# Raising the scheduling priority of the RWKV recurrence steps in a hybrid decoder layer

## Chip, cores and metric

The kernel runs on one core of a Trainium2 chip. The metric is the device time of one execution in microseconds (us); the median of three runs of the kernel before is 1586.47 us (1586.15 to 1588.06).

## What is computed

One decoder layer over 1024 tokens of width 1024, in float32. An RMS norm and one input projection feed two branches: RWKV-7 time mixing (16 heads of 64) and dilated windowed attention (16 heads of 64). Both are gated, concatenated, projected out and added to the input; a last RMS norm follows. Cut to what matters:

```python
xn = rms_norm(h, norm_w)
p = einsum('bsd,dn->bsn', xn, w_in)              # 1024 x 8320
def step(state, inp):                            # the RWKV recurrence, per head, state 64 x 64
    r_t, w_t, k_t, v_t, av_t, bv_t = inp
    sa = einsum('bhvk,bhk->bhv', state, av_t)
    state = state * w_t + sa[..., None] * bv_t + v_t[..., None] * k_t
    return state, einsum('bhvk,bhk->bhv', state, r_t)
y_rwkv = gated(group_norm(lax.scan(step, s0, xs)))
y_att = mixed_dilated_attention(p[..., ATT0:ATT_GATE0], p[..., ATT_GATE0:])
h = h + einsum('bsm,md->bsd', concat([y_rwkv, y_att]), w_out)
return rms_norm(h, final_norm_w)
```

## The kernel before

The program has three stages. In the first (to about 880 us) the RWKV branch is computed, and the projections run beside it; then comes attention, with the remaining projections beside it; last comes the output projection.

**Units and chunks.** The RWKV stage works on 16 units: 8 pairs of heads, each in two halves of 512 tokens. A unit has 8 chunks of 64 tokens. The recurrence inside a chunk is turned into matrix products, for which a triangular matrix per chunk is inverted (`invert`); what is left of the recurrence is a serial chain over the chunks (`chain`), with three steps a chunk.

- `first`: a product of the state `Sd` closes the PSUM tile `z` (I write z<-Sd), DVE copies one half of it into the tile `zd` and then ACT the other (`spread`, L654 and L655). Two more products (T<-Vd, T<-Sd) open the chunk's result tile `T`.
- `second`: the product with the inverse `U` (z<-zd); DVE and then ACT write `ud` (L657, L658).
- `third`: T<-ud closes `T`; DVE and then ACT write the next state `Sd` (L657, L658), and z<-Vd opens the next chunk's `z`.

So one chunk is the loop z<-Sd, zd, z<-zd, ud, T<-ud, Sd, in which each link waits for the one before: three products on PE (in float32, 128 columns or fewer, two passes each) and three pairs of small operations on DVE and ACT, the one on ACT after the one on DVE.

**What lies beside the chain.** While unit p goes through its chain, unit p+1 is inverted (the columns on DVE at L568 and L570, a round trip through DRAM, then the small products m1 to m4 at L596, L606, L619 and L628) and unit p+2 is prepared (decay, norms, products `pa`). Unit p-1 is finished (group norm, gate). And PE has a stream of projection products, `pq` (L187), 128x512 in float32r, 3,120 of them in all, which wait for nothing in this stage: `advance(4)` takes four of them after every slot. A unit has 24 slots, one chain step in each; other steps are assigned to slots by the tables PREP, FIN, LATE, MS.

**What sets the order.** The loop below writes out the work slot by slot. A scheduler then fixes, when the program is built, one order for each engine's queue: it takes instructions that it holds to be ready, and among these the one with the highest priority, which without further word is the place in the written order. On the chip each engine works through its queue in that order and waits by semaphores. In a slot the chain step is written first, then `finish`, `late`, `invert`, `prepare`, `products`, then four `pq`.

Of the kernel before, what the change touches and what calls it, by code (L numbers as in the profile page):

```python
# [29 lines left out]
ATTG0 = 7296  # L30
NSLOT = 3 * NC_
AHEAD = 120
OFILL = 8
WARM = (4, 0)
V_AT = (-2, 3, -1)
# [18 lines left out]
class Kern:  # L54
# [135 lines left out]
    def stream(self, jobs):  # L190
# [3 lines left out]
        for i, (_, halves, take) in enumerate(jobs):  # L194
# [9 lines left out]
                yield  # L204
            w = wn

    def advance(self, n):
        for _ in range(n):
            next(self.flow, None)
        self.taken += n  # L210
# [80 lines left out]
    def rwkv(self, pairs=range(NPAIR), apairs=range(NPAIR)):  # L291
        nc = self.nc
        with ExitStack() as ctx:
# [45 lines left out]
            get = lambda n: units[n] if 0 <= n < N else None  # L339
            self.lora_w(units[0])  # L340
            for p in range(-2, N):
                dA, dI, dC, dF = get(p + 2), get(p + 1), get(p), get(p - 1)
                ev = [[] for _ in range(NSLOT)]
                put = lambda steps: [ev[s].append(f) for s, f in steps]
                if dC:
                    put(enumerate(self.chain(dC, get(p + 1) if dC["h"] == 0 else None)))
                if dF:
                    put(self.finish(dF))
                if dI:
                    put(self.late(dI))  # L350
                    put(self.invert(dI, self.Us[(p + 1) % 2]))
                if dA:
                    lag = WARM[p + 2] if p < 0 else 0
                    put([(n + lag, f) for n, f in self.prepare(dA) + self.products(dA)])
                if get(p + 3) and get(p + 3)["h"] == 0:
                    ev[12].append(lambda d=get(p + 3): self.lora_w(d))
                elif get(p + 3):
                    get(p + 3)["lw"] = get(p + 2)["lw"]
                if p == -2:
                    px = self.prep_x(1, self.lng, tags, ba)  # L360
                    for s in range(4):
                        ev[s].append(lambda: [next(px, None) for _ in range(2)])
                    ev[4].append(lambda: [None for _ in px])
                n = 5 if p < 0 else 2 if dA is not None and get(p + 3) is None else 4
                for s in range(NSLOT):
                    for f in ev[s]:
                        f()
                    self.advance(n)
# [367 lines left out]
    def attention(self, ctx, pairs=range(NPAIR), filler=None):  # L736
# [15 lines left out]
        per = 8 * 3 * KT  # L752
        done, ahead = max(0, self.taken - self.nrwkv), min(AHEAD, per * (len(prs) - 1))

# [26 lines left out]
        for j, (pr, e) in enumerate(heads):  # L781
            nxt = heads[j + 1] if j + 1 < len(heads) else None
            todo = self.scores(nxt[1], data[nxt[0]]) if nxt else []
            if j == len(heads) - 2:
                done, rate, per, ahead = 0, OFILL, 0, -20 * OFILL * (len(prs) - 1)
                self.flow = filler if filler is not None else iter(())
# [313 lines left out]
```

## Time and profile before

| | us |
|---|---|
| median of 3 runs | 1586.47 |
| the profiled execution, its own time | 1586.58 |
| its span, first to last instruction | 1584.9 |
| PE busy in the span | 1492.5 |
| PE busy from 140 to 840 us (chain of 15 of the 16 units) | 658.29 of 700 |
| DVE, ACT busy in that stretch | 474.32, 433.42 |

How to read it: PE is the matrix engine; its products are pipelined and their ends are modelled, so a product's row is longer than the time until the next may start. DVE and ACT are the vector and the scalar engine. "Idle before" and the views of waits name what ended an engine's idle time. An engine that is not the bottleneck may be idle at no cost.

### The profile page before, as it was taken

Reading aid. Unit: us, or ns where it says so; the run is one execution under the profiler, and the core shown is the slowest. Engines: PE = TensorE matmul, PEld = TensorE weight load, DVE = VectorE, ACT = ScalarE, POOL = GpSimd, SP = SyncE. Lnnn points to the kernel's source line nnn. Section 1 sums busy time; section 2 is a strip of 40 time slices with the busy share of each in tenths; the row PEclk is TensorE's granted clock in tenths of the full one; section 3 lists DMA queues with packets and bytes.
Section 4 is the critical chain, followed back from the end, with each engine's and each line's share of the span. In section 5 each row is a group of like instructions: output and inputs, shape, how many; then the busy total and the mean of one; then the engine's idle time right before and its main releaser. Section 6 shows DMA issues by size and latency. Waiting matters only on the chain.

```text
span 1584.9 us, 29112 instructions
## 1 busy us (share of the span) xinstructions
PE 1492.5 (94%) x10721; PEld 1211.0 (76%) x10721; DVE 1014.7 (64%) x2686; ACT 892.7 (56%) x2080; POOL 532.9 (34%) x668
## 2 busy tenths in 40 slices
PE   5889999999999999999999999999999999999997
PEld 4677777777777777777677788888888888787886
DVE  5866767677666676666743557676675766856234
ACT  5546666666656666566654456556565555645231
POOL 5443132222222221232211433443333334355542
PEclk9999999999999999999999999999999999999999
DMA  6121111111111111111111201111111111436452
GB/s 195 56 67 38 34 40 42 35 45 28 39 45 33 46 39 26 47 31 45 31 40 35 68 28 34 39 50 34 34 34 41 47 48 47 157 103 193 134 166 99
DMA packets 178829, 94.87 MB, mean 60 GB/s; under 512 B 58413, under 2 KB 164606, under 8 KB 178686
## 3 DMA queue, kind: packets, MB, share of 16 engines
q1 hardware_dynamic: 174942, 86.19, 19.6%
q10 hardware_dynamic: 3744, 6.82, 1.3%
q8 instruction: 84, 1.38, 0.4%
q14 instruction: 59, 0.48, 0.1%
HBM read 75.01 MB, written 17.83 MB: 59 GB/s over the span
## 4 chain that ended last, share of the span: by engine, by line
PE 66%; DVE 18%; ACT 9%; issue 4%; POOL 1%; DMA 1%; DVEq 0%; SPq 0%; ACTq 0%; POOLq 0%
PE pq L187 31%; PE oq L984 10%; PE T L643 4%; PE z L643 3%; PE o L930 3%; PE pa L527 2%; PE mp L857 2%; PE sp L890 2%; DVE I L422 1%; PE sp L910 1%; PE sp L909 1%; ACT zt L724 1%; DVE TB L568 1%; ACT ud L658 1%; DVE UB L570 1%
## 5 line engine op out<-in xcount | busy, mean ns | idle before, releaser
L187 PE MATMUL pq<-xh,wh 128*128 128x512 f32 x1040 | 430.6, 414 | 0.0
L187 PE MATMUL pq<-xl,wh 128*128 128x512 f32 x1040 | 414.7, 399 | 0.0
L187 PE MATMUL pq<-xh,wl 128*128 128x512 f32 x1040 | 291.8, 404 | 0.0
L179 POOL TENSOR_TENSOR wl<-wraw,wh 128x512 fp32r<-128x512 f32 x138 | 181.1, 1328 | 173.9 <-issue 46.3
L187 PEld LDWEIGHTS pq<-xh,wh 128*128 128x128 f32 x1040 | 197.0, 190 | 32.6 <-issue 0.2
L187 PEld LDWEIGHTS pq<-xl,wh 128*128 128x128 f32 x1040 | 197.4, 190 | 31.2 <-DVE xl L166 0.2
L187 PEld LDWEIGHTS pq<-xh,wl 128*128 128x128 f32 x1040 | 187.8, 190 | 33.0
L918 POOL TENSOR_TENSOR pl<-p,ph 128x512 fp32r<-128x512 f32 (+2 forms) x96 | 102.0, 1068 | 202.7 <-ACT ph L917 182.4
L984 PE MATMUL oq<-ow,qr 128*128 128x512 f32 x512 | 162.2, 395 | 1.2 <-ACT ow L965 0.6
L859 DVE CUSTOM_DVE_ANT_0 mp<-mp,maskq 128x512 f32<-128x512 f32 (+1 forms) x192 | 105.5, 570 | 68.0 <-PE mp L857 59.5
L913 ACT ACTIVATE p<-p 128x512 f32<-128x512 f32 (+2 forms) x144 | 64.6, 452 | 103.8 <-DVE p L912 103.0
L979 POOL TENSOR_TENSOR vr<-kr,qr 128x512 fp32r<-128x512 f32 (+2 forms) x68 | 90.4, 1335 | 80.9 <-ACT qr L978 74.0
L984 PEld LDWEIGHTS oq<-ow,qr 128*128 128x128 f32 x512 | 95.9, 188 | 23.0 <-ACT ow L965 1.0
L984 PE MATMUL oq<-ow,vr 128*128 128x512 f32 x256 | 101.2, 395 | 1.9 <-POOL vr L979 1.9
L178 ACT CAST wh<-wraw 128x512 fp32r<-128x512 f32 x138 | 79.7, 618 | 40.6 <-PE pq L187 30.9
L978 ACT CAST qr<-kr 128x512 fp32r<-128x512 f32 (+2 forms) x68 | 40.2, 594 | 94.3 <-PE oq L984 53.1
L912 DVE TENSOR_TENSOR p<-sp,maskt 128x512 f32<-128x512 f32 (+2 forms) x144 | 65.3, 457 | 42.9 <-PE sp L910 41.4
L643 PEld LDWEIGHTS T<-ud,TU 128*128 128x128 f32 x256 | 39.6, 188 | 56.2 <-ACT ud L658 51.8
L643 PE MATMUL T<-ud,TU 128*128 128x128 f32 x256 | 59.4, 314 | 22.7 <-ACT ud L658 22.1
L657 DVE TENSOR_SCALAR Sd<-T,dec 64x64 f32<-64x64 f32 x120 | 33.0, 275 | 66.8 <-PE T L643 65.0
L658 ACT ACTIVATE ud<-z,rn 64x64 f32<-64x64 f32 x128 | 39.4, 308 | 56.5 <-DVE ud L657 54.9
L658 ACT ACTIVATE Sd<-T,dec 64x64 f32<-64x64 f32 x120 | 36.9, 308 | 57.0 <-DVE Sd L657 55.6
(235 smaller groups left out, 3126.6 us busy)
## 6 DMA issues: line engine op xcount, KB each, us to landing
wraw<-in_w_in_dram SPq DMA_DIRECT2D x138, 256.0 KB, 3.0
kr<-mixd SPq DMA_DIRECT2D x60, 256.0 KB, 3.0
oraw<-in_w_out_dram SPq DMA_DIRECT2D x16, 512.0 KB, 5.2
xt<-in_x_dram SPq DMA_DIRECT2D x8, 512.0 KB, 3.8
ld<-TU SPq DMA_DIRECT2D x32, 128.0 KB, 2.7
mixd<-zt SPq DMA_DIRECT2D x16, 256.0 KB
mixd<-gt SPq DMA_DIRECT2D x16, 256.0 KB, 2.2
xr<-in_x_dram ACTq DMA_DIRECT2D x16, 256.0 KB, 2.8
```

The costliest lines, as they stand in the source:

```text
L178: nc.scalar.copy(out=wh[:, ks], in_=raw)
L179: nc.gpsimd.tensor_tensor(out=wl[:, ks], in0=raw, in1=wh[:, ks].bitcast(F32), op=ALU.subtract)
L187: return [lambda i=i, a=a, b=b: self.nc.tensor.matmul(q, lhsT=a, rhs=b, start=(i == 0), stop=(i == len(ops) - 1)) for i, (a, b) in enumera ...
L643: mm = lambda out, w, x, start, stop: nc.tensor.matmul(out, lhsT=w, rhs=f2(x), start=start, stop=stop, skip_group_check=True)
L658: S.activation(out=out[er[1], 1], in_=q[0:64, 64:128], func=AF.Copy, scale=scale[1])
L859: V.tensor_tensor_reduce(out=mp[:, :kn], in0=mp[:, :kn], in1=self.maskq[:, v0:v0 + kn], op0=ALU.add, op1=ALU.max, scale=1.0, scalar=-3e38, ...
L912: V.tensor_tensor(out=p[:, :qn], in0=sp[:, :qn], in1=self.maskt[:, u0:u0 + qn], op=ALU.add)
L913: S.activation(out=p[:, :qn], in_=p[:, :qn], func=AF.Exp)
L918: G.tensor_tensor(out=pl[:, :qn], in0=p[:, :qn], in1=ph[:, :qn].bitcast(F32), op=ALU.subtract)
L930: nc.tensor.matmul(oc, lhsT=v, rhs=w[:, :qn], start=(first and i == 0), stop=(last and i == len(prods) - 1), skip_group_check=True)
L979: nc.gpsimd.tensor_tensor(out=ml, in0=raw, in1=mh.bitcast(F32), op=ALU.subtract)
L984: nc.tensor.matmul(q, lhsT=m[:, i], rhs=v, start=(k == 0 and j == 0), stop=(k == 15 and j == 2))
```

## The change

Each step of `chain` is called through a new helper, `urgent`, which raises the priority of everything that the step issues by 90 places of the written order (a slot has about 30 instructions). No instruction is added, removed or resized; only the order within the queues is another.

```diff
 AHEAD = 120
+AHEAD_OF = 90
...
+    def urgent(self, f):
+
+        with self.tc.high_priority(offset=AHEAD_OF):
+            f()
...
                 if dC:
-                    put(enumerate(self.chain(dC, get(p + 1) if dC["h"] == 0 else None)))
+                    for s, f in enumerate(self.chain(dC, get(p + 1) if dC["h"] == 0 else None)):
+                        ev[s].append(lambda f=f: self.urgent(f))
```

What it does to the queues is shown at three places of one unit, the seventh (first half of the fourth pair of heads); the twelve inner units are alike. Line numbers of the changed kernel are higher by 1 to 7.

**Place A.** PE, chunk 1: from z<-Sd to z<-zd; `tq` are four transposes for the next unit, `pq` projections. Before:

```order
L643 MATMUL z<-Sd_123,AR_142 66x128
L643 MATMUL T_4772<-Vd_120,MV 128x128
L643 MATMUL T_4772<-Sd_123,AR_142 128x128
L496 MATMUL tq<-ident,BK 128x128 x4
L187 MATMUL pq<-xh_78,wh 128x512
L187 MATMUL pq<-xl_80,wh 128x512
L187 MATMUL pq<-xh_78,wh 128x512
L187 MATMUL pq<-xl_80,wh 128x512
L643 MATMUL z<-zd_127,U_118 66x128
```

In the changed kernel PE has this there:

```order
L650 MATMUL z<-Sd_123,AR_142 66x128
L650 MATMUL T_4772<-Vd_120,MV 128x128
L650 MATMUL T_4772<-Sd_123,AR_142 128x128
L503 MATMUL tq<-ident,BK 128x128 x2
L650 MATMUL z<-zd_127,U_118 66x128
```

The four projections and two of the transposes that stood between the two products of the chain now stand behind the second.

**Place B.** PE, chunk 6: from z<-zd to T<-ud; `x` and `xq` are small products of the next unit's inversion. Before:

```order
L643 MATMUL z<-zd_126,U_118 66x128
L187 MATMUL pq<-xh_79,wh 128x512
L187 MATMUL pq<-xl_81,wh 128x512
L187 MATMUL pq<-xh_79,wh 128x512
L187 MATMUL pq<-xl_81,wh 128x512
L619 MATMUL x_5284<-UT,TU 32x32 x3
L643 MATMUL T_5082<-ud_128,TU 128x128
```

In the changed kernel:

```order
L650 MATMUL z<-zd_126,U_118 66x128
L603 MATMUL xq<-U_119,LT 16x16 x30
L650 MATMUL T_5082<-ud_128,TU 128x128
L650 MATMUL z<-Vd_120,MV 66x128
L603 MATMUL xq<-U_119,LT 16x16 x2
L188 MATMUL pq<-xh_78,wl 128x512 x5
```

Four projections gave place to 30 tiny products of the first step of the inversion.

**Place C.** DVE, from the state after chunk 0 to the `zd` of chunk 1; `rs`, `gr`, `rn` and `nq` belong to norms of other units, `TB` and `UB` to the inversion. Before:

```order
L657 TENSOR_SCALAR Sd_123<-T_4772,dec 64x64
L67 TENSOR_SCALAR rs_x<-gs 128x8
L568 TENSOR_TENSOR TB<-UB,AB 64x15
L68 TENSOR_SCALAR rs_w<-rs_x 128x8
L570 TENSOR_TENSOR UB<-UB,TB 64x15
L443 TENSOR_REDUCE nq<-sqt 128x8
L70 TENSOR_SCALAR gr<-rs_w 128x8
L72 TENSOR_SCALAR rs_x<-rs_x 128x8
L447 TENSOR_SCALAR rn<-nq 64x4 x4
L77 TENSOR_TENSOR rs_w<-gr 128x8
L654 COPY zd_127<-z 64x64
```

In the changed kernel:

```order
L664 TENSOR_SCALAR Sd_123<-T_4772,dec 64x64
L575 TENSOR_TENSOR TB<-UB,AB 64x63
L577 TENSOR_TENSOR UB<-UB,TB 64x9x7
L575 TENSOR_TENSOR TB<-UB,AB 64x60
L577 TENSOR_TENSOR UB<-UB,TB 64x10x6
L661 COPY zd_127<-z 64x64
```

The copy of the chain has passed the reductions and the norms; in the changed kernel 31 other operations stand instead between `zd` and `ud` of chunk 0.

## Rows read from the trace of the kernel before

**Rows 1.** The page's first part: busy time, share, instructions of each engine.

```profile
span 1584.9 us, 29112 instructions
...
PE 1492.5 (94%) x10721; PEld 1211.0 (76%) x10721; DVE 1014.7 (64%) x2686; ACT 892.7 (56%) x2080; POOL 532.9 (34%) x668
...
```

**Rows 2.** Busy time of the engines from 140 to 840 us (second number: the stretch).

```profile
core 0: us, PE busy (x) PEld busy (x) DVE busy (x) ACT busy (x) POOL busy (x), PEclk, DMA share, GB/s
140.00:840.00 700.00, 658.29 (x6474) 515.64 (x6472) 474.32 (x1462) 433.42 (x1143) 174.53 (x298) 1.00 0.16 37
```

**Rows 3.** Waits of PE over the span: total us, times, longest.

```profile
engine line waited for: us in total, times, longest us
PE T L643 <- ACT ud L658: 22.1, 39, 1.0
...
PE z L643 <- ACT zd L655: 9.2, 11, 1.3
...
PE z L643 <- ACT Sd L658: 7.4, 15, 0.7
```

**Rows 4.** Timeline, chunks 6 and 7: start, duration, engine, line, operation.

```profile
450.93 0.39 PE L643 MATMUL z<-Sd,AR 128*66 128x128 f32 x2
451.36 0.22 DVE L654 COPY zd<-z 64x64 f32<-64x64 f32 x1 [0.87 <-PE z L643]
451.61 0.20 ACT L655 COPY zd<-z 64x64 f32<-64x64 f32 x1 [0.78 <-DVE zd L654]
451.89 0.43 PE L643 MATMUL z<-zd,U 128*66 128x128 f32 x2
452.26 0.58 PE L596 MATMUL xq<-U,LT 32*16 32x16 f32 x52
452.37 0.28 DVE L657 TENSOR_SCALAR ud<-z,rn 64x64 f32<-64x64 f32 x1 [0.79 <-PE z L643]
452.68 0.31 ACT L658 ACTIVATE ud<-z,rn 64x64 f32<-64x64 f32 x1 [0.86 <-DVE ud L657]
...
459.18 0.49 PE L643 MATMUL T<-ud,TU 128*128 128x128 f32 x2
459.71 0.28 DVE L657 TENSOR_SCALAR Sd<-T,dec 64x64 f32<-64x64 f32 x1 [0.92 <-PE T L643]
460.02 0.31 ACT L658 ACTIVATE Sd<-T,dec 64x64 f32<-64x64 f32 x1 [0.89 <-DVE Sd L657]
```

**Rows 5.** Timeline, chunks 0 and 1 of the same unit, same columns.

```profile
418.43 0.38 PE L643 MATMUL z<-Sd,AR 128*66 128x128 f32 x2
418.64 0.39 PE L643 MATMUL T<-Vd,MV 128*128 128x128 f32 x2
418.72 0.69 DVE L705 TENSOR_REDUCE gs<-Y 128x8 f32<-128x512 f32 x1 [0.23 <-ACT Y L695]
419.51 0.75 DVE L223 SCALAR_TENSOR_TENSOR ks<-pq,om,shtmp 128x512 f32<-128x512 f32 x1
420.18 0.21 DVE L654 COPY zd<-z 64x64 f32<-64x64 f32 x1
421.91 0.63 ACT L709 ACTIVATE ysq<-Y 128x512 f32<-128x512 f32 x1 [0.56 <-ACT MV L501]
422.56 0.31 ACT L658 ACTIVATE ud<-z,rn 64x64 f32<-64x64 f32 x1
422.92 0.49 PE L643 MATMUL T<-ud,TU 128*128 128x128 f32 x2 [0.70 <-ACT ud L658]
425.38 0.60 PE L496 MATMUL tq<-ident,BK 128*128 128x128 f32 x4
428.26 0.31 ACT L658 ACTIVATE ud<-z,rn 64x64 f32<-64x64 f32 x1 [0.63 <-DVE ud L657]
428.62 0.49 PE L643 MATMUL T<-ud,TU 128*128 128x128 f32 x2 [0.32 <-ACT ud L658]
```

**Rows 6.** The chain that ended last, one run of projections: start, length, what.

```profile
884.16 20.66 PE pq L187 x91
```

## The prediction

> **What bounds the kernel now.** I read the engines' busy times first. PE is busy 1492.5 of 1584.9 us, the next engine, DVE, 1014.7 [rows 1]. So PE sets the time, and since the change takes no product away, only PE's idle time can change. In the stretch of the chain, 140 to 840 us, PE is busy 658.29 of 700 us at full granted clock: 41.7 us are idle, and DVE and ACT are far from full (474.32 and 433.42) [rows 2]. The view of waits says what ends those gaps: T<-ud waits for ACT's `ud` 22.1 us in 39 waits, z<-zd for `zd` 9.2 us in 11, z<-Sd for `Sd` 7.4 us in 15, together 38.7 us in 65 of 384 chain steps [rows 3]. The rest of PE's idle time lies in the load of x, at the start of attention and at the end, which the change does not touch. So the prize is at most 38.7 us, 2.4%.
>
> What makes such a wait is seen in the timeline. There are two sides to it, the latency of a link and the cover, which is the work that stands on PE between the two products of the chain.
>
> Latency without a queue, from the start of one product to the next that may start [rows 4]: z<-Sd at 450.93, DVE at 451.36 (0.43), 0.22 long, ACT 0.03 after it, 0.20 long; and PE starts 0.05 after ACT's end (428.26 + 0.31 = 428.57, PE at 428.62) [rows 5]. That is 0.93 us for `zd`. In the same way 0.48 + 0.28 + 0.03 + 0.31 + 0.05 = 1.15 us for `ud`, and 0.53 + 0.28 + 0.03 + 0.31 + 0.05 = 1.20 us for `Sd` [rows 4]. I call these the floors. A chunk cannot go round in less than 3.3 us.
>
> With a queue it is longer: z<-Sd at 418.43 could have had its copy at 418.86, but DVE first did `gs` (0.69) and `ks` (0.75), and copied at 420.18, 1.3 us late; `ud` on ACT waited behind `ysq` (0.63), and T<-ud then kept PE idle for 0.70 us [rows 5]. These two mechanisms, a queue on DVE or ACT and too little cover on PE, are what the change shifts.
>
> **What it removes.** The chain's operations pass others on DVE and ACT. At place C ten operations, `nq` with the largest among them, stood between `Sd` and `zd`, now four small ones. But the work that is passed does not vanish: it stands elsewhere between two chain operations. To weigh this I took every chunk of the stage (127 intervals from one T<-ud to the next) and added up, from the order, what each engine has between the corresponding operations, with durations from the trace. For PE I used pitches: 0.23 us for a `pq` (20.66 / 91) [rows 6], about 0.22 for a two-pass chain product (418.43 to 418.64), 0.11 for a transpose (0.15 with the modelled tail, 0.60 / 4 [rows 5]; I estimate 0.11 as half a two-pass product), at most 0.011 for a pass of `xq` (0.58 / 52) [rows 4, 5]. Before: PE 645 us, DVE 524, ACT 464. In 48 chunks DVE or ACT has more than PE, by 39.2 us together. The trace's own figure for the chain's waits is 38.7 [rows 3], so this count sizes them well. After: in 51 chunks, 35.5 us. So by this count only 3.7 us of queue go. The excess now sits in chunk 0 (DVE 8.26 us against PE's 7.68, the 31 operations ahead of `ud`), chunk 1 (4.58 against 3.58) and chunk 4 (7.45 against 7.20), where before it sat in chunks 0, 1 and 3 (7.22 against 6.19 in the last). (PE's sum falls to 627 since the last unit's chain ends earlier among the projections; the products are the same.)
>
> **What it adds.** The chain's products stand as early on PE as the scheduler held them to be ready, and so the cover shrinks. At place A the cover was two T products, four transposes and four pq, 1.94 us with the z product itself; now it is 3 x 0.22 + 2 x 0.11 = 0.89, just under the floor of 0.93. At place B it was 1.37 us for a floor of 1.15; now there is the z product and 30 tiny products of two passes. With the passes' modelled length that is 0.37 (451.89 to 452.26) + 60 x 0.011 = 1.03 us [rows 4]; start to start over the stage they come closer, and I count 0.73. So PE must stand still for 0.1 to 0.4 us in every unit (I take 0.42; with the other end the sum below falls by 16 x 0.3 = 5 us). The five pq that could fill it stand behind T<-ud, and PE takes its queue in order. Over all 368 steps with a floor (the first state of a unit has no such link): before, 45 steps have less cover than the floor, by 3.9 us together; after, 152 steps, by 25.5 us: `zd` 44 steps and 3.5 us, `ud` 50 and 15.2, `Sd` 58 and 6.8.
>
> **Sum.** The two overlap, since a chunk that is late through DVE does not lose the shortage too. So for each chunk I take the largest of PE's sum plus its shortage, DVE's sum and ACT's sum. Over PE's own sum that gives 41.3 us before and 56.5 us after: 15.2 us more. By chunk of a unit after: 0.71, 1.00, 0.41, 0.19, 0.34, 0.16, 0.45, 0.39; before 0.49, 0.99, 0.19, 1.02, 0.01, 0.10, 0.05, 0.02. The profiled execution took 1586.58 us, 0.1 from the median, and becomes 1586.6 + 15.2 = **1601.8 us**.
>
> **Costed at nothing.** The chain issues no DMA, and SP's queue keeps its pattern in every unit (two weight loads, `ld`, `AB`, two loads, `ud`, `U`, a store), so the weights for the projections come as before; POOL, a quarter busy in the stage (174.53 of 700) [rows 2], keeps its work within a unit. If a weight came late, PE would show a wait at L187, of which the list of waits has none today. PE now goes from other products into a run of tiny ones 32 times more often; after z<-zd `xq` starts 0.37 us later instead of about 0.22 [rows 4, 5], so that this may cost 32 x 0.15 = 4.8 us. Some of these changes fall into gaps that are counted above, so I leave it in the range and out of the sum.
>
> What the Trainium skill says on this: TensorE: Matmul & The Clock Gate, in the section on the array's architectural detail, states that ACT and DVE are strict first-in-first-out, and that PE's queue can only pull weight loads ahead. That speaks against the change, since a product placed too early blocks what follows; `ud` behind `ysq` and the idle 0.70 us on PE agree [rows 5].
>
> **Rivals.**
>
> *The waits go (faster).* If the order meets the engines as the scheduler meant it, DVE and ACT are free when the chain asks, and the 35.5 us of queue do not appear. For it speaks that the total is small for both engines (68% and 62% busy [rows 2]) and that an early chain gives later steps slack: chunks 0, 4 and 6 have over 6 us of PE work for a loop of 3.3. Against it, the same excess in the counts of both kernels. Then only the shortage stays: 1586.6 - 38.7 + 25.5 = 1573 us; with partial success 1565 to 1583.
>
> By the Perfetto Trace Analysis page of the Trainium skill (section Optimization Strategy), one finds the gaps on the bound engine and makes what they wait for start sooner. If all the chain's gaps closed, that would be 1586.6 - 38.7 = 1548 us; I hold this for a small part of the rival's chance, since the shortage is in the order itself.
>
> *A trade at par (same).* Queue saved equals cover lost: 1587 us. By the count that takes 21.6 us of queue removed rather than 3.7.
>
> *Late links without cover (much slower).* The mechanism: with cover at the floor, any operation in progress on ACT or DVE (0.6 to 0.75 us long [rows 5]) goes straight to PE's idle time, which the wide cover absorbed before. The place is every newly short step, 152 - 45 = 107. If each lost what a wait of T<-ud costs now, 22.1 / 39 = 0.57 us, the loss is 61 us: 1648 us. It decides when these operations start off the scheduler's time by more than about 0.2 us.
>
> *No effect.* The order is in fact another on PE, DVE and ACT (places A to C), so this is excluded as such.
>
> **How the numbers follow.** My forecast (1590 to 1618) has 0.45, the much slower case 0.10, par 0.15, the waits go 0.30. A measurement of this kernel can tell about 0.2%, 3.2 us, from no change: faster 0.30, same 0.15, slower 0.55. The range reaches from most of the second-best case, 1566, to halfway from forecast to the much slower one, 1630; about 0.06 is left out below and 0.09 above.
>
> **What would show it.** In the profile after: PE's waits on `ud`, `zd` and `Sd` up from 38.7 to about 54 us, with many more and shorter ones (over 100 instead of 65); T<-ud after xq in chunk 6 with 0.4 us idle in each unit; DVE and ACT busy sums unchanged; the first to last chain product no longer apart than now. Wrong would be: these waits below 35 us (the queue was the cause, and it goes), or waits that moved to the inversion's or the preparation's products (L527, L619, L628), which the count takes as ready.

## The result, and the profile after

The changed kernel takes 1601.83 us (median of 4 runs, 1599.32 to 1606.61) against 1587.26 us before (median of 4, 1586.15 to 1588.06). The ratio is 1.0096, with a 95% interval of 1.0067 to 1.0125: slower by about 1%, and clear of no change. The forecast was 1601.8 us. The four runs of the changed kernel lie 7 us apart, so an agreement to 0.03 us is luck.

The first part of the page of the changed kernel, as in [rows 1], and its stretch from 140 to 840 us, as in [rows 2]:

```profile
span 1597.7 us, 29109 instructions
...
PE 1514.3 (95%) x10721; PEld 1211.8 (76%) x10721; DVE 1007.2 (63%) x2686; ACT 892.1 (56%) x2080; POOL 556.0 (35%) x668
```

```profile
140.00:840.00 700.00, 666.04 (x6233) 507.81 (x6233) 464.57 (x1455) 427.98 (x1124) 196.65 (x298) 1.00 0.16 37
```

PE is busy 21.8 us longer with the same 10721 instructions (behind every x, each of the two passes of a float32 product counts as one; a `pq` and a transpose have one pass). In 700 us it does 6233 of them where it did 6474, and yet it is busy for longer, at the same full clock. The new time is therefore not in what the profile counts as idle. The waits of PE say the same; this is the view of [rows 3], for the changed kernel (the lines of `ud`, `Sd` and `zd` are 7 further down now):

```profile
PE T L650 <- ACT ud L665: 11.2, 25, 1.6
PE pa L534 <- DVE BK L470: 10.3, 7, 4.2
PE z L650 <- ACT Sd L665: 7.4, 22, 1.5
PE z L650 <- ACT zd L662: 6.7, 14, 0.8
PE x L626 <- DVE UT L618: 3.7, 7, 0.6
```

The chain's waits fell from 38.7 us in 65 to 11.2 + 7.4 + 6.7 = 25.3 us in 61. The total came out as forecast, but these waits went the other way. So the time must lie in rows that count as busy. One part of it is still waiting, too short to be listed: in 152 links before and 235 after, the chain's product starts within 0.08 us of the end of ACT's copy, and so was held up by it. The view lists 65 and 61 of them, since the modelled end of the product before hides a short hold-up, or leaves a gap of under 0.15 us. The first product of attention starts at 904.66 us before and at 918.28 after, and from there the two kernels stay the same distance apart to within 1 us: all of the loss lies in the RWKV stage. For that stage (118.7 to 904.6 us before, 117.3 to 918.2 after) the groups of PE by line and operation show it. The two numbers behind the bar are busy us and mean ns of one. Before:

```profile
L527 PE MATMUL pa<-AR,BK 64*128 64x128 f32 x448 | 47.0, 289 | 2.3 <-ACT MV L533 1.9
L496 PE MATMUL tq<-ident,BK 128*128 128x128 f32 x120 | 18.2, 273 | 0.0
L596 PE MATMUL xq<-U,LT 32*16 32x16 f32 x960 | 11.3, 174 | 0.0
L606 PE MATMUL dq<-Xs,UT 16*16 16x16 f32 x1008 | 10.9, 175 | 0.0
```

and after:

```profile
L534 PE MATMUL pa<-AR,BK 64*128 64x128 f32 x448 | 53.7, 296 | 2.3 <-DVE BK L470 2.2
L503 PE MATMUL tq<-ident,BK 128*128 128x128 f32 x120 | 20.4, 272 | 0.0
L613 PE MATMUL dq<-Xs,UT 16*16 16x16 f32 x1000 | 16.0, 173 | 0.4 <-ACT Xs L606 0.4
L603 PE MATMUL xq<-U,LT 32*16 32x16 f32 x960 | 13.5, 174 | 0.0
```

One pass lasts as long as before (175 and 173 ns for `dq`, 273 and 272 for `tq`), but a group as a whole is busy longer: 5.1 us more for `dq`, 6.7 for `pa`, 2.2 for `xq` and for `tq`. Products of one group overlap as long as they stand in a row: 64 passes of `dq` take 0.69 us below, though one lasts 0.17. The chain's products now break these rows up. The timeline shows it. PE before, around one step of `dq` (start, duration):

```profile
407.39 0.39 PE L643 MATMUL T<-Vd,MV 128*128 128x128 f32 x2
407.62 0.39 PE L643 MATMUL T<-Sd,AR 128*128 128x128 f32 x2
407.94 0.69 PE L606 MATMUL dq<-Xs,UT 16*16 16x16 f32 x64
408.55 0.50 PE L187 MATMUL pq<-xh,wh 128*128 128x512 f32 x1
```

and the same step after, in three pieces:

```profile
416.22 0.38 PE L650 MATMUL z<-zd,U 128*66 128x128 f32 x2
416.53 0.37 PE L613 MATMUL dq<-Xs,UT 16*16 16x16 f32 x28
416.82 0.49 PE L650 MATMUL T<-Vd,MV 128*128 128x128 f32 x2
417.24 0.21 PE L613 MATMUL dq<-Xs,UT 16*16 16x16 f32 x2
417.38 0.49 PE L650 MATMUL T<-Sd,AR 128*128 128x128 f32 x2
...
418.46 0.41 PE L613 MATMUL dq<-Xs,UT 16*16 16x16 f32 x34
```

From T<-Vd to T<-Sd it took 0.23 us before (407.39 to 407.62). After, with one product of `dq` (two passes) between them, it is 0.56 (416.82 to 417.38). In a run of 64 passes such a product costs 0.61 / 32 = 0.02 us (407.94 to 408.55). So this single break costs 0.31 us, and none of it is shown as a wait.

To book the whole stage in this way I took each product's interval from its start to the next one's start, subtracted the least that its kind takes (the tenth percentile before the kind of neighbour that follows soonest; about 550 us in all, the same in both kernels), and put the rest down to the kind of the product that came next. "Tiny" are `xq`, `dq` and `x` of the inversion. A "run" is a row of products of one kind with no other between them, and an entry is its first product. A wait for an input falls into the column of the product that waited. In us, for every kernel of this study (the experiments follow below; the kernel before had medians of 1585.2 to 1586.8 beside them, so the ratios there carry the verdicts):

| kernel | median | runs of tiny products / pa | chain link (z<-zd, T<-ud, z<-Sd) | entry to tiny | entry to pa | z<-Vd, T<-Vd, T<-Sd | pq | stage |
|---|---|---|---|---|---|---|---|---|
| before | 1587.3 | 83 / 41 | 72.2 | 13.7 | 10.1 | 41.8 | 50.6 | 786.1 |
| the change | 1601.8 | 115 / 67 | 71.2 | 24.6 | 16.2 | 48.5 | 46.2 | 801.1 |
| e1 copies only | 1584.2 | 78 / 28 | 67.6 | 12.3 | 5.9 | 41.5 | 52.1 | 783.9 |
| e2 tiny in three | 1632.9 | 180 / 41 | 83.3 | 35.8 | 9.5 | 42.0 | 61.1 | 832.0 |
| e3 far ahead | 1592.5 | 64 / 57 | 80.1 | 15.5 | 8.2 | 47.4 | 48.2 | 792.4 |
| e4 chain, inversion, pa | 1618.1 | 105 / 28 | 98.1 | 28.1 | 5.9 | 47.1 | 43.5 | 822.9 |
| e5 products only | 1618.5 | 131 / 53 | 93.7 | 23.1 | 14.9 | 46.4 | 49.3 | 819.6 |
| e6 chain and tiny | 1624.6 | 120 / 88 | 92.8 | 34.3 | 15.2 | 47.8 | 45.1 | 831.0 |
| e7 copies, inversion, pa | 1592.8 | 65 / 28 | 68.5 | 22.9 | 6.2 | 42.3 | 49.2 | 797.5 |
| e8 pa in four | 1602.0 | 85 / 82 | 73.2 | 14.5 | 20.9 | 41.2 | 58.6 | 800.8 |
| e9 last eight slots | 1597.0 | 93 / 41 | 81.5 | 15.4 | 9.4 | 43.4 | 48.7 | 797.5 |
| e10 first ten slots | 1590.5 | 83 / 34 | 67.7 | 15.6 | 11.9 | 46.9 | 51.1 | 793.3 |
| e11 copies, slots 2 to 9 | 1574.1 | 78 / 29 | 61.2 | 12.4 | 10.9 | 45.1 | 49.4 | 774.5 |

The stage grows by 15.0 us (it also starts 1.4 us sooner). Of these, the entries to tiny products bring 10.9, those to pa 6.1, the chain's other products 6.7, together 23.7; the links take back 1.0, `pq` 4.4, and the rest (not listed) about 3. With other choices of the kinds the single columns move by up to 5 us, while the sum of these three stays between 20 and 25.

That the entries grow by the breaks, and not by inputs that come late, can be seen when the entries that take up a step already begun are counted by themselves: 34 before with 6.4 us, 105 after with 23.4 us; those that begin a step stay at 18 us. And of z<-Vd, T<-Vd and T<-Sd, 43 now stand right behind a tiny product or `pa`, none before. The links lose only 1.0 us although 13.4 us of listed waits are gone: so about 12 of the 21.8 us of new busy time are hold-ups at links that no longer show as waits.

### The profile page after: what moved, and what is told of

The parts are those of the page before. It is cut to its first block, busy times and chain, and to the rows that moved or that the text cites. A ratio compares the mean times of both kernels' runs of the same rounds, so it can differ in the third digit from the quotient of the medians.

```text
span 1597.7 us, 29109 instructions
## 1 busy us (share of the span) xinstructions
PE 1514.3 (95%) x10721; PEld 1211.8 (76%) x10721; DVE 1007.2 (63%) x2686; ACT 892.1 (56%) x2080; POOL 556.0 (35%) x668
## 4 chain that ended last, share of the span: by engine, by line
PE 70%; DVE 15%; ACT 9%; issue 3%; POOL 1%; DMA 1%; DVEq 0%; SPq 0%; ACTq 0%; POOLq 0%
PE pq L188 33%; PE oq L991 10%; PE T L650 5%; PE z L650 5%; PE o L937 3%; PE pa L534 3%; PE mp L864 2%; PE sp L897 2%; DVE TB L575 2%; DVE I L429 1%; PE sp L917 1%; ACT zt L731 1%; DVE UB L577 1%; PE sp L916 1%; ACT Sd L665 1%
## 5 line engine op out<-in xcount | busy, mean ns | idle before, releaser
L188 PE MATMUL pq<-xl,wh 128*128 128x512 f32 x1040 | 420.4, 404 | 0.0
L180 POOL TENSOR_TENSOR wl<-wraw,wh 128x512 fp32r<-128x512 f32 x138 | 187.6, 1377 | 279.7 <-PE pq L188 124.7
L991 PEld LDWEIGHTS oq<-ow,qr 128*128 128x128 f32 x512 | 96.5, 189 | 23.1 <-ACT ow L972 1.1
L179 ACT CAST wh<-wraw 128x512 fp32r<-128x512 f32 x138 | 79.5, 616 | 35.6 <-PE pq L188 25.0
L664 DVE TENSOR_SCALAR ud<-z,rn 64x64 f32<-64x64 f32 x128 | 35.2, 275 | 78.6 <-PE z L650 77.4
L661 DVE COPY zd<-z 64x64 f32<-64x64 f32 x128 | 27.1, 212 | 72.7 <-PE z L650 71.8
L650 PE MATMUL T<-ud,TU 128*128 128x128 f32 x256 | 59.1, 313 | 13.6 <-ACT ud L665 11.2
```

Source lines behind the costliest of these rows:

```text
L179: nc.scalar.copy(out=wh[:, ks], in_=raw)
L180: nc.gpsimd.tensor_tensor(out=wl[:, ks], in0=raw, in1=wh[:, ks].bitcast(F32), op=ALU.subtract)
L188: return [lambda i=i, a=a, b=b: self.nc.tensor.matmul(q, lhsT=a, rhs=b, start=(i == 0), stop=(i == len(ops) - 1)) for i, (a, b) in enumera ...
L650: mm = lambda out, w, x, start, stop: nc.tensor.matmul(out, lhsT=w, rhs=f2(x), start=start, stop=stop, skip_group_check=True)
L991: nc.tensor.matmul(q, lhsT=m[:, i], rhs=v, start=(k == 0 and j == 0), stop=(k == 15 and j == 2))
```

## The experiments

Two theories were put against each other: links without cover, which is the forecast's, and changes of kind, which the trace after suggests. Each is worked out from the order of a kernel before it ran. All ratios below are against the kernel before.

### Pricing a break by itself: e2 and e8

Without raised priority, the steps of tiny products (e2) and of pa (e8) are broken up by `pq` products, whose number stays the same. The edits to the kernel before, in m1 to m4 and in the step of pa (in e8, too, the three `pq` are taken off the slot's own):

```diff
         for c in range(NC_):
+                if c in (2, 5):
+                    self.advance(1)
...
-                    self.advance(n)
+                    self.advance(n - 2 if dI and s in MS else n)
```

```diff
             for b in range(4):
...
+                if b in (0, 1, 2):
+                    self.advance(1)
```

> The kernel before, without any raised priority, but each of the inversion's four steps (16 tiny products) is broken in three by one pq product after the third and the sixth pair; these pq are taken from the step's own allowance, so their number is unchanged. 180 runs of tiny products instead of 83, pa unchanged at 41. Links without cover: 89 short steps with 8.0 us, sum of the largest per chunk 49.2 against 41.1, so 8 us more, about 1595. Changes of kind: 97 entries more by 0.26 us are 25 us more, about 1612; if only the first product of a run is late and not the one after it, half of that, 1600.

> The kernel before, without raised priority, but each step of eight pa products is broken in four by one pq each time, these pq taken from the step's own allowance. 82 runs of pa instead of 41 and 85 of tiny products instead of 83. Links without cover: 53 short steps with 4.4 us, sum of the largest per chunk 46.3 against 41.1: 5 us more, about 1592. Changes of kind: 43 entries more, by the 0.35 us of the tiny products 15 us, about 1602; if going over to pa (64-row weights, 128 columns) is cheaper, nearer to 1592.

e2: 1632.85 us, ratio 1.0292 (1.0278 to 1.0306). e8: 1602.01 us, 1.0101 (1.0087 to 1.0115). The page's row of the engines and the group of `dq` in the stage for e2, then the same row and the group of `pa` for e8:

```profile
PE 1528.1 (94%) x10721; PEld 1212.3 (74%) x10721; DVE 1019.5 (62%) x2686; ACT 894.0 (55%) x2080; POOL 543.2 (33%) x668
```

```profile
L608 PE MATMUL dq<-Xs,UT 16*16 16x16 f32 x1024 | 14.8, 174 | 0.0
```

```profile
PE 1507.8 (94%) x10721; PEld 1212.6 (76%) x10721; DVE 1013.4 (63%) x2686; ACT 891.1 (56%) x2080; POOL 529.8 (33%) x668
```

```profile
L527 PE MATMUL pa<-AR,BK 64*128 64x128 f32 x448 | 53.2, 300 | 4.0 <-ACT MV L535 3.9
```

With 97 runs more, PE's busy time is 35.6 us longer in e2: 0.37 us for each break, not the 0.26 that I had expected. In e8 it is 15.3 us for 41 runs of pa more, again 0.37 (0.36 with the two more runs of tiny products). Both cost far more than the links' shortage (8 and 5 us) can explain: e2 lost 46 us against the kernel before, and e8 16.8 us where the changes of kind gave 15. This shows that a break costs time when `pq` makes it too, and not only the chain, and that the cost is booked as busy time, both on the way in (the entries in the table, 13.7 to 35.8 in e2) and on the way out (`pq`, 50.6 to 61.1).

### The halves of the change: e1 and e5

e1 raises only the two copies of each chain step, e5 only the chain's products; the step as a whole is no longer raised in either:

```diff
         def spread(out, q, scale):
+            self.urgent(lambda: spread_(out, q, scale))
```

```diff
-        mm = lambda out, w, x, start, stop: nc.tensor.matmul(out, lhsT=w, rhs=f2(x), start=start, stop=stop,
-                                                             skip_group_check=True)
+        mm = lambda out, w, x, start, stop: self.urgent(lambda: nc.tensor.matmul(
+            out, lhsT=w, rhs=f2(x), start=start, stop=stop, skip_group_check=True))
```

> Only the chain's two copies (DVE and ACT) are emitted with the raised priority; its products on TensorE are left to follow in their own order. Two theories for the 15 us that the whole change costs in the RWKV stage. Links without cover (the forecast's): the time is the shortage of cover between the chain's products. By the order there are 41 short steps with 3.3 us (45 with 3.9 before), and the sum of the largest per chunk is 44.0 us against 41.1: 2.9 us more, about 1590 against 1587.3. Changes of kind: the time is what TensorE loses whenever it goes over to the 16-wide products of the inversion (xq, dq, x) or to the preparation's pa; 58 such entries more in the whole change for 15 us are 0.26 us each. Here the tiny products form 78 runs (83 before) and pa 28 (41 before), 18 entries fewer: 4.7 us less, about 1582.6. So 1590 or 1583.

> The other half of the change: only the chain's products on TensorE are emitted with the raised priority, its two copies are not. Links without cover: 168 short steps with 23.8 us, and the copies now come late besides; the sum of the largest per chunk is 77.6 us against 41.1, 36.5 more, about 1623. Changes of kind, now at the 0.35 us per entry that the kernel with the inversion in three pieces shows in TensorE's own time (35.6 us of busy time more for 97 runs more): 131 runs of tiny products and 53 of pa, 60 entries more than before, 21 us, about 1608.

e1: 1584.17 us, 0.9986 (0.9977 to 0.9995). e5: 1618.52 us, 1.0209 (1.0193 to 1.0225). The copies alone are a small gain, 2.6 us, where the 18 missing runs were to give 4.7 and the links to cost 2.9. The products alone cost more than twice what the whole change does: 14.2 us at the entries (17.0 in the change), and 21.5 us at the links, where the waits on `zd` and `Sd` are 17.6 and 14.6 us: with the copies not raised, the two halves of a step come apart. The forecasts were 36.5 for the links and 21 for the entries; the time lies between them.

### Which slots cost: e9 and e10

The change, with the chain raised only in part of a unit's 24 slots (`s >= 16` in e9, `s < 10` in e10):

```diff
-                        ev[s].append(lambda f=f: self.urgent(f))
+                        ev[s].append((lambda f=f: self.urgent(f)) if s >= 16 else f)
```

> The change, but only the chain's steps of slots 16 to 23 of each unit (the slots in which the inversion's tiny products are emitted) are raised. By the order this has almost all of the change's shortage at the links and few of its changes of kind, so it tells the two apart. Links without cover: 157 short steps with 24.0 us (152 with 25.5 in the change), sum of the largest per chunk 61.1 against 41.1, 20 us more: about 1606. Changes of kind: 93 runs of tiny products and 41 of pa, 10 entries more than before, by 0.35 us 3.5 us more: about 1590.

> The change, but only the chain's steps of slots 0 to 9 of each unit are raised, where no tiny product and no pa is emitted. Links without cover: 103 short steps with 10.0 us, sum of the largest per chunk 43.5 against 41.1: about 1589. Changes of kind: 83 runs of tiny products and 34 of pa, 7 entries fewer than before: about 1584.5. If what the change gains in waits on ud (22.1 us before, 11.2 after) comes without its price in entries, the time falls further, to 1575 to 1580.

e9: 1596.99 us, 1.0069 (1.0056 to 1.0083). e10: 1590.45 us, 1.0025 (1.0015 to 1.0035). PE's waits on the chain in e9, then in e10:

```profile
PE T L650 <- ACT ud L665: 23.9, 37, 1.0
...
PE z L650 <- ACT zd L662: 13.5, 27, 1.1
...
PE z L650 <- ACT Sd L665: 2.7, 6, 0.5
```

```profile
PE z L650 <- ACT zd L662: 12.2, 10, 1.9
PE z L650 <- ACT Sd L665: 10.0, 26, 1.5
PE T L650 <- ACT ud L665: 6.5, 21, 0.6
```

e9 has 94% of the change's shortage (24.0 of 25.5 us) and 10 entries more than before, and it loses 9.3 us at the links, less than half of the 20 forecast, while its entries cost 1.0 more. So links without cover do cost, and that part of the forecast's theory stands. e10 shows where a gain lies: raised in the first ten slots, T<-ud waits 6.5 us instead of 22.1 [rows 3]. It isn't faster for this. Other waits grew (`zd` by 3.0 us, `Sd` by 2.6, and `pa` for `BK` from 8.1 to 13.0), and so did the chain's other products (5.1 us) and the entries (3.7); the clock may have a part in it (last section).

### Keeping the broken steps together: e3, e4, e6, e7

e3 raises the chain by 200 instead of 90. The others raise the inversion's steps too, so that they stay together: e4 chain, m1 to m4 and pa; e6 chain and m1 to m4; e7 copies, m1 to m4 and pa. The first edit is that of e3; of the second, which is e4's, e6 has the lower part alone, and e7 has it with e1's:

```diff
-AHEAD_OF = 90
+AHEAD_OF = 200
```

```diff
-        steps = [(PROD + 2 * c4, lambda c4=c4: step(c4)) for c4 in range(2)]
+        steps = [(PROD + 2 * c4, lambda c4=c4: self.urgent(lambda: step(c4))) for c4 in range(2)]
...
-    (LT, lt)] + list(zip(MS, (m1, m2, m3, m4)))
+    (LT, lt)] + [(s, lambda f=f: self.urgent(f)) for s, f in zip(MS, (m1, m2, m3, m4))]
```

> The whole change, but raised by 200 instead of 90, so the chain stands still further ahead of the other work. Links without cover: 177 short steps with 16.4 us, sum of the largest per chunk 51.0 against 41.1: 10 us more than before, about 1597. Changes of kind: 64 runs of tiny products (83 before, 115 in the change) and 57 of pa (41 and 67), 3 entries fewer than before: about 1586.5, 15 us faster than the change as it is.

> The whole change, and the steps of the inversion (xq, dq, x) and of the preparation that issue tiny products and pa are raised by the same 90, so that the chain's products break them up less. Links without cover: 153 short steps with 14.4 us, sum of the largest per chunk 55.4 against 41.1, nearly that of the change (56.3): about 1601. Changes of kind: 105 runs of tiny products and 28 of pa, 9 entries more than before and 49 fewer than in the change: 2.3 us more than before, about 1589.6.

> The whole change, and the inversion's four steps of tiny products are raised by the same 90; pa is not. Links without cover: 134 short steps with 14.5 us, sum of the largest per chunk 41.9 against 41.1: about 1588. Changes of kind: 120 runs of tiny products and 88 of pa, 84 entries more than before, by 0.35 us 29 us more, about 1616. If the inversion's raised products instead stand ahead of the transposes and copies that they need, TensorE's waits on ud, zd, Sd and Xs show it: over 50 us together as in the kernel with the inversion and pa raised.

> Raised priority for the chain's copies, the inversion's four steps and the preparation's pa, but not for the chain's products. Links without cover: 64 short steps with 5.7 us, sum of the largest per chunk 52.4 against 41.1: 11 us more, about 1598. Changes of kind: 65 runs of tiny products and 28 of pa, 31 entries fewer than before, by 0.35 us 11 us less, about 1576, the fastest of all.

e3: 1592.53 us, 1.0040 (1.0026 to 1.0053). With the runs back at 64 and 57 its entries cost what they did before (23.7 against 23.8 us, of which 7.7 are waits of `x` for `UT`), 17 us less than with the change; what is left is the links, 7.9 us more, and the chain's other products, 5.6. e3 is the change with most of its breaks undone, and the time goes from 1601.8 to 1592.5, about halfway between the two theories.

e4: 1618.09 us, 1.0203 (1.0189 to 1.0217). e6: 1624.61 us, 1.0244 (1.0227 to 1.0261). e7: 1592.84 us, 1.0050 (1.0037 to 1.0062). e4 and e6 are slower than either theory gives, and e7 is slower than the changes of kind give. In e7 the waits name the reason: the raised inversion stands ahead of what it needs.

```profile
PE dq L613 <- ACT Xs L606: 5.3, 13, 0.5
PE x L626 <- DVE UT L618: 5.3, 14, 0.6
```

These 10.6 us, absent before, take the place of the 11 that the fewer runs were to give. In e4 most of the loss lies at the links (25.9 us more than before, entries 10.2); in e6 the entries cost 25.7 us more, near the 29 forecast, and the links 20.6. PE's waits in e4:

```profile
PE T L650 <- ACT ud L665: 39.0, 34, 2.4
...
PE z L650 <- ACT zd L662: 10.6, 28, 1.7
...
PE z L650 <- ACT Sd L665: 5.8, 18, 0.6
```

That is 55.4 us against 38.7. In e6 it is 42.0, or 45.1 with `Xs`, so the 50 us expected there didn't come. 30 of e4's 55.4 us are 13 waits of T<-ud, of 2.2 to 2.4 us each. What stands on DVE ahead of `ud` there is not a raised step but the inversion's columns and an operation of the preparation. Around one of the 13, DVE and POOL:

```profile
383.48 2.53 POOL L180 TENSOR_TENSOR wl<-wraw,wh 128x512 fp32r<-128x512 f32 x2 [4.32 <-PE pq L188]
384.87 1.20 DVE L575 TENSOR_TENSOR TB<-UB,AB 64x55 f32<-64x55 f32 x1
386.11 0.21 DVE L577 TENSOR_TENSOR UB<-UB,TB 64x55 f32<-64x55 f32 x1
387.37 0.27 DVE L664 TENSOR_SCALAR ud<-z,rn 64x64 f32<-64x64 f32 x1
```

Beside POOL's `wl` a column operation takes 1.20 us, and the next of the same size 0.21. In both kernels, too, every operation of the columns that lasts over 0.3 us (20 before, 25 after) runs beside an operation of POOL, nearly always `wl`, and takes up to 1.25 us; without POOL beside it, none of them takes over 0.22. That POOL holds them up is not shown by an experiment. In e4 and e6 the clock took time as well (last section); what they would be at a steady clock stays open.

### A version that is faster than both: e11

The copies are raised throughout as in e1, the chain's products only in slots 2 to 9, away from the tiny products:

```diff
+                        ev[s].append((lambda f=f: self.urgent(f)) if 2 <= s < 10 else f)
```

> The chain's copies raised throughout, its products only in slots 2 to 9: the version that by both counts should be the fastest. Links without cover: 82 short steps with 8.2 us, sum of the largest per chunk 46.6 against 41.1: about 1592. Changes of kind: 78 runs of tiny products and 29 of pa, 17 entries fewer than before, 6 us less: about 1581, with the waits on ud also fewer than in the kernel with the copies alone (27.0 us).

1574.05 us, 0.9921 (0.9909 to 0.9933): 0.8% faster than before and 1.7% faster than the change. Its page and its waits:

```profile
span 1573.2 us, 29077 instructions
...
PE 1487.9 (95%) x10721; PEld 1204.5 (77%) x10721; DVE 1011.5 (64%) x2686; ACT 893.2 (57%) x2080; POOL 539.6 (34%) x668
```

```profile
PE T L650 <- ACT ud L668: 17.0, 30, 1.1
...
PE z L650 <- ACT zd L665: 7.8, 9, 1.5
...
PE z L650 <- ACT Sd L668: 2.0, 8, 0.4
```

The chain's waits are 26.8 us, nearly as low as with the change (25.3), while PE is busy 26.4 us less than there: the gain of the change with few of its breaks (78 and 29 runs). It is better than either sum, since neither had the fall of the waits in it.

## Why the prediction was right, and where it was not

The total was right, 1601.8 for 1601.83 us; the way to it was not. Two errors made up for each other: some 21 us too little was taken off at the links, and the breaks, 23.7 us in the table, were left out.

**What bounds the kernel** (PE, in the RWKV stage) held. **That PE only idles or works at a fixed cost** did not: "since the change takes no product away, only PE's idle time can change" is the sentence that failed. Its busy time rose by 21.8 us with the same products. The view of groups by line could have told: `xq` took 11.3 us for 960 passes, 12 ns each, though one lasts 174. The prediction used that pitch (0.011 us), but priced the way into a run at 0.15 us and the way out of it at nothing.

**What it adds**: the shortage at the links was sized well. I split all links by the order, into those with less cover than the floor and the others, and took by how much the link's second product came later than such a step usually does. The short ones, 45 before and 152 after, were late by 9.5 us before and 32.8 after: 23.3 us more for the 21.6 forecast (25.5 - 3.9). Most of this doesn't show as a wait, so the forecast of 54 us in the list of waits failed all the same. At place B the 0.4 us of idle time per unit, which the sum took, didn't come. The rows of the trace after that answer [rows 4]:

```profile
411.68 0.38 PE L650 MATMUL z<-zd,U 128*66 128x128 f32 x2
411.99 0.65 PE L603 MATMUL xq<-U,LT 32*16 32x16 f32 x60
412.41 0.31 ACT L665 ACTIVATE ud<-z,rn 64x64 f32<-64x64 f32 x1 [1.86 <-DVE ud L664]
412.77 0.49 PE L650 MATMUL T<-ud,TU 128*128 128x128 f32 x2
```

z to T takes 1.09 us. T<-ud starts 0.05 us after the end of `ud` (412.41 + 0.31 = 412.72), so it does wait for it; but PE is idle for only 0.13 us (411.99 + 0.65 = 412.64 to 412.77), too little to be listed, and the same in 13 units. So the cover was near the other end that the prediction named (1.03 us) and not 0.73.

**What it removes** is the term that was mis-sized: 3.7 us of queue. By the same count, links with enough cover were late by 43.1 us before (323 of them) and by 18.1 after (216): 25.0 us less. Part of this is that 107 links went over to the short ones, where the forecast counted their shortage on top. So the links together give -1.0 us (table), where the sum had +15.2. The rival "the waits go" had this point right, and gave 1573. Raised steps of the first ten slots (e10) let the links fall by 4.5 us, raised copies (e1) by 4.6, and e11, which has both in the main, by 11.0; which operations on DVE and ACT bring it stays open.

Some of the prediction's working doesn't come out of its own figures: place C has twelve operations between `Sd` and `zd`, not ten; the cover at place A adds up to 2.02 us, not 1.94, by the pitches given; and the list by chunk gives 0.78 us a unit more, 12.5 us for 16 units, where the sum has 15.2.

**Costed at nothing, or left in the range**: 32 more entries to tiny products by 0.15 us, 4.8 us, out of the sum. They measured 10.9 us in the table; a break priced by itself costs 0.37 (e2, e8). The 26 more runs of pa, 6.1 us, were not seen at all, nor the 6.7 us of z<-Vd, T<-Vd and T<-Sd. Without this left-out term, 23.7 us, the stage would have become shorter, and not 15.0 us longer. DVE's and ACT's sums are unchanged to 1%, as said (1007.2 and 892.1 us), and SP's queue kept its order but for five pairs of neighbours among 573 transfers.

**What would show it**: "these waits below 35 us" stood there as a sign of being wrong, and they are 25.3. Waits also moved to `x` (3.7 us on `UT`) as the other sign named. Read before the time, these two lines would have pointed to the faster rival; the busy row is what contradicts it. Two more signs failed: the list has 61 waits, not over 100, and from the first to the last product of the chain it is 764.0 us instead of 747.1, though it was to be no longer.

The Trainium skill's page Perfetto Trace Analysis (section Optimization Strategy) says to find the gaps of the bound engine and make what they wait for start sooner. The change did so, and the gaps shrank by 13.4 us; the time grew by 14.6. In e11, where the earlier work hardly breaks up what the engine does at a stretch, the gaps shrank by 11.9 us and the time by 12.2.

## What to carry to other kernels

Before moving work forward on the bound engine, count not only its idle time but the runs of equal products that the moved ones cut: here small products, which overlap at 12 ns a pass, cost 0.3 to 0.4 us for each cut, and the profile books that as busy time. Compare the busy sum at an equal count of instructions before reading the waits: a list of waits that gets shorter can mean that they became too short to be listed. Raise the priority of the short operations on the engines that aren't the bound, and of the bound engine's own only where nothing small is being run.

## What the runs showed of the hardware that I had not expected

A wait of PE can cost more than its length, by the clock. In e4, T<-ud waits some 2.3 us in 13 units, since DVE has other operations in front of `ud`. PE around one such wait, and the granted clock of the same stretch (the third number from the end):

```profile
385.21 0.39 PE L188 MATMUL pq<-xh,wh 128*128 128x512 f32 x1
388.03 0.80 PE L650 MATMUL T<-ud,TU 128*128 128x128 f32 x2 [2.44 <-ACT ud L665]
```

```profile
386.00:388.00 2.00, 0.00 (x0) 0.00 (x0) 1.83 (x9) 0.31 (x1) 0.10 (x2) 1.00 0.64 185
388.00:390.00 2.00, 1.97 (x8) 1.79 (x9) 0.90 (x5) 0.31 (x1) 0.00 (x0) 0.50 0.26 77
390.00:392.00 2.00, 2.00 (x13) 1.90 (x12) 0.49 (x2) 0.20 (x1) 0.42 (x2) 0.64 0.14 33
```

From 388.0 to about 391.4 the clock is at 0.50 (1.2 GHz), and T<-ud takes 0.80 us instead of 0.49. Each such episode takes 1.7 us of PE's work (2 x 0.50 + 2 x 0.36); that is the most that it can cost, and an estimate. It doesn't follow every wait: the one of 2.34 us that ends at 337.47 leaves the clock at 1.00. Between 120 and 920 us there is none before (where z<-zd waits 1.25 us in three units), one with the change (at 135 us, behind a wait of 1.5 us for `Sd`; 1.7 us), nine in e4 (15.4 us; eight follow one of the 13 waits), five in e10 (8.5 us, for waits of 1.5 and 1.86 us), and 20.5 us in e6; e3, e7, e9 and e11 have one each, and e5 two. In e9 the wait ahead of it was 1.1 us, and in e5 no wait of 1 us or more stands close ahead.

The time doesn't follow this count in full. The four runs of e6 had mean clocks of 0.979, 0.981, 0.983 and 0.987 and took 1626.93, 1626.20, 1623.02 and 1620.12 us: 6.8 us less, where the clock alone would make it 0.008 x 1626 = 13 us. The run of e10 with the highest clock, 0.994, took 1587.81 us, still more than the kernel before beside it (1586.23), so the clock alone doesn't explain why e10 is no gain.
